# Two groups of stores in a one-layer encoder step: prepared w_out operands stored from ScalarE's queue one step behind, partial outputs stored right behind each pair's last sum

## The chip, the cores and the metric

The kernel runs on one core of a Trainium2 chip. The metric is the device time of one launch in microseconds. Each number on the profile is from one profiled execution of that launch.

The core has five engines that run their own instruction streams in order: TensorE (PE; its weight loads are listed apart as PEld), VectorE (DVE), ScalarE (ACT), GpSimd (POOL) and SyncE (SP). SP, ACT and POOL can start DMA transfers. An engine that issues a transfer waits in its own stream until the data to be moved is ready.

## The reference, cut to what matters

One layer of an encoder over 4096 prompt rows and 32 sample rows of width 1024, in float32:

```python
h = rmsnorm(x, norm_g)
u, v, z_a, xb, z_b = jnp.split(h @ w_in, 5, axis=-1)               # each 1024 wide
a = u * chunk_mlp(layernorm(v), w_spatial, b_spatial) * silu(z_a)  # 8 heads, 128 x 128 mixing
b = pool_mix(xb_with_past, ...) * silu(z_b)                        # trailing windows 2, 4, 8, 16
y = x + concat([a, b], -1) @ w_out                                 # w_out is 2048 x 1024
return rmsnorm(y, final_g), ...                                    # and three small states
```

## The kernel before, in words

All large products are Strassen-like: a product of two-by-two blocks is made of seven block products (q = 0 to 6) in place of eight. Each operand is split in a rounded upper half and the rest (hi and lo), and a block product is 12 matmuls: four blocks of the contraction, each hi x hi, hi x lo and lo x hi. One block product is called a step here.

The program has three stages.

1. Norms, the v columns, and the operands made of the normalised rows. The operands go to DRAM (`xops`), the v rows to `v_all`.
2. Four groups of 1024 tokens, each with 16 sets of 128 columns: 8 gate sets (z and u) and 8 pooling sets (x_B folded with the pooling weights, and z_B). The results, branch outputs transposed, go to DRAM (`abT`).
3. The product with w_out, in two halves of its rows: z = 0 for branch a, z = 1 for branch b. A pair is 256 token rows. The 16 pairs of z = 0 write partial sums to DRAM (`part`), the 16 pairs of z = 1 read them back, add, normalise and write the output. The last two pairs of z = 0 keep their sums on chip for the first two of z = 1.

In stages 2 and 3 the operands that the matmuls take as weights are made on the fly. `prepare` runs through the list of steps five ahead of the multiplication (`LEAD = 5`). For each step it issues due loads and then runs the step's preparation: ACT rounds the block to hi (line 120), DVE subtracts to get lo (line 82), and for some q DVE forms sums first (line 116). Each operand lies in a buffer `wop`, of which there are seven. ACT also copies block products out of PSUM (lines 168, 173 and 175), and DVE adds others (line 166).

w_out's own operands (class `OutWeights`, one for each half z and row block k, so eight of them with seven operands each, 56 in all) are prepared during stage 2, beside a step's own preparation, one every second or every third step. They too go through a `wop` buffer and are then stored to DRAM (`wops`), from which stage 3 loads them. The store is issued by SP right behind the preparation (line 631), in the same queue as the loads of raw weights (line 897) and v rows (line 890). The buffer is free when the store has landed.

In stage 3 a pair's sums lie in two tiles `y`. After the last step of a pair, DVE adds the last product (line 703). `finish` stores `y` to `part` from POOL (line 714); before the change it is called in the third step of the next pair, and for the first pair right behind its own last step.

The order in which the instructions of each engine stand is not the order of the code alone: a scheduler places them by its own estimate of when each is ready, engine by engine, and a few are held in the order of the code (`keep_in_program_order`).

Of the kernel before, what the change touches and what calls it, by code (L numbers as in the profile page):

```python
# [8 lines left out]
F32 = mybir.dt.float32  # L9
# [22 lines left out]
NQ = 7  # L32
# [4 lines left out]
def stream_step(ctx: ExitStack, tc, x_prompt, x_sample, state_pool, norm_g, w_in, ln_v_g, ln_v_b,  # L37
# [9 lines left out]
    nc = tc.nc  # L47
# [30 lines left out]
    def small(tag, n, rows=P):  # L78
        return smallp.tile([P, 8], F32, tag=tag, name=tag)[:rows, :n]
# [32 lines left out]
    def weight_ops(a1, a2, b1, b2, sums, dst, in_order=False):  # L112


        keep = {}
        less = lambda o, x, y: nc.vector.tensor_tensor(o, x, y, ALU.subtract)  # L116

        def split(q, src):
            hi, lo, *then = dst(q)
            pair = nc.scalar.copy(hi, src), lo_part(lo, src, hi)  # L120
            if q == 0 and in_order:
                for ins in pair:
                    tc.keep_in_program_order(ins)
            if behind:
                behind.pop()
                tc.keep_in_program_order(pair[0])
            for step in then:
                step()

        def third():  # L130
            keep[1], keep[2] = sums(), sums()
            less(keep[1], b1, a1)
            less(keep[2], b2, keep[1])
            split(2, keep[2])

        def fourth():
            less(b1, b2, b1)
            split(3, b1)

        def last():  # L140
            less(a2, a2, keep[2])
            split(6, a2)

        return [lambda: split(0, a1), lambda: split(1, a2), third, fourth, lambda: split(4, keep[1]),
                lambda: split(5, b2), last]
# [67 lines left out]
    def pool(name, bufs, stack=ctx, **kw):  # L213
        return stack.enter_context(tc.tile_pool(name=name, bufs=bufs, reuse_waits="tile", **kw))
# [4 lines left out]
    with ExitStack() as ph:  # L219
# [138 lines left out]
        class Past:  # L358


            def load(self):
                self.st = half(), half()
                for z in range(2):
                    nc.gpsimd.memset(self.st[z][:HALO], 0.0)
                    nc.sync.dma_start(self.st[z][1:HALO], state_pool[0, 0, :, z * 512:(z + 1) * 512])
# [234 lines left out]
    def raw_tile(dt=F32):  # L600
        return raw_p.tile([P, D], dt, tag="raw", name="raw")

    def weight_tile():
        return op_p.tile([P, 2, 4, P], F32R, tag="wop", name="wop")
# [6 lines left out]
    def load_out_weights(z, q):  # L611
        w_slots[z, q] = t = slot()[:, :4 * D].rearrange("p (k h n) -> p k h n", k=4, h=2)
        nc.sync.dma_start(t.bitcast(F32), wops[z, q].rearrange("p k (h n) -> p k h n", h=2))

    class OutWeights:


# [3 lines left out]
        def load(self):  # L621
            v = []
            for i in range(2):
                raw = raw_tile()
                nc.sync.dma_start(raw, w_out_v[8 * self.z + 4 * i + self.k])
                v.append(raw.rearrange("p (s c e) -> p s c e", s=2, e=P))

            def dst(q):
                t = weight_tile()
                out = wops[self.z, q, :, self.k, :]  # L630
                store = lambda: nc.sync.dma_start(out, t.rearrange("p h k t -> p (h k t)").bitcast(F32))
                return t[:, 0], t[:, 1], store

            self.prep = weight_ops(v[0][:, 0], v[1][:, 0], v[0][:, 1], v[1][:, 1], sum_tile, dst)

# [172 lines left out]
    with ExitStack() as ph:  # L808
# [225 lines left out]
        groups = []  # L1034
# [4 lines left out]
        n_sets = len(groups)  # L1039
# [23 lines left out]
        def prepare(upto):  # L1063

            nonlocal done
            while done < min(upto, len(steps)):
                while loads and loads[0][0] <= done + (AHEAD if done < first[id(groups[n_sets][0])] + 7 else 6):
                    loads.pop(0)[2].load()
                s, q = steps[done]
                s.prep[q]()  # L1070
                if done in beside:
                    w, q = beside[done]
                    w.prep[q]()
                done += 1
# [25 lines left out]
        for n in range(n_sets):  # L1100
            g, order = groups[n], orders[n]
# [48 lines left out]
    with ExitStack() as ph:  # L1150
        y_p = pool("y_p", 6, ph)
        ps_more = pool("ps_more", 2, ph, space=bass.MemoryType.PSUM)

        def y_tile():
            return y_p.tile([P, D], F32, tag="y", name="y")

        def more_tile():
            return ps_more.tile([P, 512], F32, tag="more", name="more")

        def spare_tile():  # L1160
            return spare_p.tile([P, D], F32, tag="spare", name="spare")


        def sum_words():
            return sum_p.tile([P, 512], F32, tag="sum", name="few")

        def few_columns():
            t = sum_words()
            return [t[:, i * DEC:(i + 1) * DEC] for i in range(2)]

        state = FewRows(lambda k: stk[:, k * m_edge + EXT:(k + 1) * m_edge],
                        lambda k: w_in[0, k * P:(k + 1) * P, 3 * D:4 * D], few_columns, KT // 2 - 1)
        outs = FewRows(lambda k: abT[k, :, SEQ:], lambda k: w_out_v[k], few_columns, KT - 1)

        def state_end():
            low = raw_tile()
            few_sums(low[:DEC], state.acc, sum_words)
            nc.sync.dma_start(st_prompt[0, 0], low[DEC - POOL_STATE:DEC])
            nc.sync.dma_start(st_sample[0, 0], low[EXT - POOL_STATE:EXT])

        def outs_end():
            y, low = raw_tile()[:DEC], raw_tile()[:DEC]
            nc.sync.dma_start(y, xs)
            few_sums(low, outs.acc, sum_words)
            nc.vector.tensor_tensor(y, low, y, ALU.add)
            ss, a = small("nb", 1, DEC), small("na", 1, DEC)
            junk = sum_p.tile([P, 2 * 512], BF16, tag="sum", name="junk")[:DEC]
            nc.scalar.activation(junk, y, AF.Square, accum_out=ss)
            nc.vector.tensor_scalar(a, ss, 1.0 / D, EPS, ALU.mult, ALU.add)
            r = rsqrt(a, 1, DEC)  # L1190
            nc.vector.scalar_tensor_tensor(y, y, r, f_bc[:DEC], ALU.mult, ALU.mult)
            nc.gpsimd.dma_start(ys, y)

        def sample_rows():

            vs, gb, bb = [raw_tile()[:DEC] for _ in range(3)]
            nc.sync.dma_start(vs, v_smp)
            nc.sync.dma_start(gb, ln_v_g[0].partition_broadcast(DEC))
            nc.sync.dma_start(bb, ln_v_b[0].partition_broadcast(DEC))
            nc.vector.tensor_tensor(gb, vs, gb, ALU.mult)  # L1200
            nc.vector.tensor_tensor(gb, gb, bb, ALU.add)
            nc.gpsimd.dma_start(v_sample[0, 0], gb)

        aside = {n_sets + 4 + 2 * j: (state, j, state_end) for j in range(4)}
        aside.update({n_sets + i: (outs, j, outs_end) for j, i in enumerate((5, 7, 9, 11, 17, 19, 21, 23))})
        kept, ended = [], None
        for n in range(n_sets, len(groups)):
            g, order = groups[n], orders[n]
            for s in g if n > n_sets else ():
                s.begin(kept.pop(0) if kept else None)  # L1210
            if g[0].z and ended is None:
                f_bc = spare_tile()
                nc.sync.dma_start(f_bc, final_g.partition_broadcast(P))
            for m, (s, q) in enumerate(order):
                at += 1
                prepare(at + LEAD)
                if m == 0 and n in aside:
                    aside[n][0].load(aside[n][1])
                if n == n_sets + 12 and m == 2:
                    sample_rows()  # L1220
                s.multiply(q)
                if n == n_sets and s is g[0] and q == NQ - 1:
                    s.finish()
                if m == 2 and ended:
                    for x in ended:
                        x.finish()
                if s is g[-1] and n + 1 < len(groups) and groups[n + 1][0].stage != s.stage:
                    load_out_weights(1, q)
                if m == 6 and n in aside:
                    few, j, end = aside[n]  # L1230
                    few.multiply(j, more_tile() if j == 0 else None)
                    if j == few.last:
                        end()
            ended = g[1:] if n == n_sets else g
            if g[0].z == 0 and groups[n + 1][0].z == 1:
                kept, ended = [x.y for x in g], None


# [27 lines left out]
```

## Time and profile before

| | |
|---|---|
| time, median of 3 runs | 2337.78 us (2337.70 to 2338.09) |
| profiled execution, its own time | 2337.89 us |
| its span, first to last instruction | 2336.0 us |
| PE busy | 2317.2 us (99%) |
| DVE busy | 1774.6 us (76%) |
| ACT busy | 889.3 us (38%) |
| POOL busy | 229.2 us (10%) |
| mean granted TensorE clock | 0.999 |
| stores of w_out's operands (line 631) | 56 of 512 KB, in SP's queue |
| stores of partial outputs (line 714) | 28 of 512 KB, in POOL's queue |

Busy shares are means over stages that have different limits. A group row gives busy time, the mean duration of one instruction, and the idle time of the engine ahead of it with what ended that. A wait is put down to what came last. A DMA row gives the time of its issue on the engine, and in the chain of waits the time until it landed. Idle time of an engine that nothing waits for costs nothing.

### The profile page before, as it was taken

To read this page: it belongs to the slowest core of one execution; us is meant where nothing else is said; L and a number is where in the kernel's file an instruction comes from. 1 tells how busy PE (TensorE), PEld (TensorE's weight loads), DVE (VectorE), ACT (ScalarE), POOL (GpSimd) and SP (SyncE) were. 2 spreads that over 40 slices of the span, in tenths; PEclk is the share of its full clock that TensorE was granted. 3 is DMA by queue.
4 is the path that set the end of the run, shared out by engine and by line. 5 is a ranking of instruction groups with operands and counts; after the bars stand their busy time and mean duration, and the time that the engine had idled before them with its cause. 6 is when DMAs were issued, how large, how long until landed. Compare 5 with 4: busy or idle time off the path is not lost.

```text
span 2336.0 us, 32648 instructions
## 1 busy us (share of the span) xinstructions
PE 2317.2 (99%) x11936; PEld 1964.7 (84%) x11936; DVE 1774.6 (76%) x3285; ACT 889.3 (38%) x1596; POOL 229.2 (10%) x412
## 2 busy tenths in 40 slices
PE   8999999999999999999999999999999999999998
PEld 7888888888888888888877899999988777887887
DVE  6888777867887777868668877768776666588887
ACT  7544444334433333433334333334322222233343
POOL 1010000100112000111001211102110000000000
PEclk9999999999999999999999999999999999999999
DMA  8879977335447433483454474435584656846552
GB/s 316 310 269 280 281 244 251 111 108 189 145 170 271 147 127 130 129 328 120 164 164 149 165 276 146 143 94 173 192 323 163 211 201 198 342 163 202 178 167 91
DMA packets 329544, 457.42 MB, mean 196 GB/s; under 512 B 21964, under 2 KB 249932, under 8 KB 326696
## 3 DMA queue, kind: packets, MB, share of 16 engines
q1 hardware_dynamic: 277832, 366.91, 46.9%
q0 software_dynamic: 22288, 73.48, 8.4%
q10 hardware_dynamic: 29264, 14.94, 2.3%
q8 instruction: 94, 1.54, 0.3%
q14 instruction: 66, 0.54, 0.1%
HBM read 286.07 MB, written 169.21 MB: 195 GB/s over the span
## 4 chain that ended last, share of the span: by engine, by line
PE 94%; DMA 3%; DVE 2%; issue 1%; ACT 0%; SPq 0%; DVEq 0%; ACTq 0%
PE acc L194 64%; PE acc L691 8%; PE acc L692 8%; PE acc L693 8%; PE sp L939 2%; PE tr L452 1%; DMA wops<-wop 1%; DMA vt<-in_w_in_dram 1%; DVE wop L82 1%; DMA raw<-abT 1%; PE more L202 1%; DMA op<-in_w_in_dram 0%; PE acc L269 0%; PE acc L202 0%; DMA raw<-in_w_in_dram 0%
## 5 line engine op out<-in xcount | busy, mean ns | idle before, releaser
L194 PE MATMUL acc<-slot,wop 128*128 128x512 f32 (+1 forms) x6720 | 1260.1, 348 | 2.9 <-ACT t L173 1.0
L194 PEld LDWEIGHTS acc<-slot,wop 128*128 128x128 f32 x6720 | 1080.3, 188 | 163.2 <-DVE t L166 6.2
L82 DVE TENSOR_TENSOR wop<-raw,wop 128x512 fp32r<-128x512 f32 x520 | 355.8, 686 | 99.0 <-ACT wop L120 96.3
L120 ACT CAST wop<-raw 128x512 fp32r<-128x512 f32 x360 | 222.8, 622 | 349.2 <-PE acc L194 259.7
L691 PE MATMUL acc<-slot,wop 128*128 128x512 f32 x892 | 348.7, 391 | 1.8 <-DVE y L703 1.8
L693 PE MATMUL acc<-slot,wop 128*128 128x512 f32 x892 | 347.1, 389 | 0.0
L692 PE MATMUL acc<-slot,wop 128*128 128x512 f32 x892 | 347.0, 389 | 0.0
L194 PE MATMUL acc<-slot,op 128*128 128x512 f32 x1344 | 323.5, 395 | 0.1
L194 PEld LDWEIGHTS acc<-slot,op 128*128 128x128 f32 x1344 | 247.6, 188 | 51.8 <-DVE op L82 0.5
L703 DVE TENSOR_TENSOR y<-acc,y 128x512 f32<-128x512 f32 x235 | 159.1, 687 | 128.0 <-PE acc L693 126.9
L166 DVE TENSOR_TENSOR t<-acc,t 128x512 f32<-128x512 f32 (+1 forms) x320 | 185.7, 582 | 85.8 <-ACT t L175 44.9
L691 PEld LDWEIGHTS acc<-slot,wop 128*128 128x128 f32 x892 | 167.4, 188 | 47.0 <-ACT wop L656 11.9
L656 ACT CAST wop<-raw 128x512 fp32r<-128x512 f32 x160 | 99.6, 622 | 259.7 <-PE acc L693 251.9
L693 PEld LDWEIGHTS acc<-slot,wop 128*128 128x128 f32 x892 | 167.4, 188 | 35.2
L692 PEld LDWEIGHTS acc<-slot,wop 128*128 128x128 f32 x892 | 167.5, 188 | 34.2
L82 DVE TENSOR_TENSOR wop<-sum,wop 128x512 fp32r<-128x512 f32 x208 | 142.5, 686 | 57.6 <-ACT wop L120 57.0
L952 POOL DMA_DIRECT2D abT<-t x128 | 69.2, 541 | 822.3 <-DVE t L964 607.9
L120 ACT CAST wop<-sum 128x512 fp32r<-128x512 f32 x144 | 89.4, 622 | 152.6 <-PE acc L194 98.4
L975 DVE TENSOR_TENSOR t<-t 128x527 f32<-128x527 f32 (+3 forms) x160 | 111.0, 697 | 0.5
L656 ACT CAST wop<-sum 128x512 fp32r<-128x512 f32 x64 | 39.9, 623 | 131.6 <-PE acc L693 102.4
L116 DVE TENSOR_TENSOR sum<-raw 128x512 f32<-128x512 f32 x72 | 49.5, 687 | 36.8 <-DMA raw<-in_w_in_dram 34.9
L175 ACT COPY t<-acc 128x512 f32<-128x512 f32 (+1 forms) x80 | 40.1, 503 | 91.0 <-PE acc L194 90.5
(199 smaller groups left out, 1866.1 us busy)
## 6 DMA issues: line engine op xcount, KB each, us to landing
raw<-in_w_in_dram SPq DMA_DIRECT2D x110, 512.0 KB, 4.3
xops<-op SPq DMA_DIRECT2D x72, 512.0 KB, 5.7
abT<-t POOLq DMA_DIRECT2D x128, 256.0 KB, 3.7
raw<-abT SPq DMA_DIRECT2D x64, 512.0 KB, 4.7
slot<-xops SPq DMA_DIRECT2D x30, 1024.0 KB, 9.6
wops<-wop SPq DMA_DIRECT2D x56, 512.0 KB, 3.3
slot<-wops SPq DMA_DIRECT2D x14, 2048.0 KB, 9.9
xt<-in_x_prompt_dram SPq DMA_DIRECT2D x32, 512.0 KB, 4.4
```

The costliest lines, as they stand in the source:

```text
L82: return nc.vector.tensor_tensor(out, src, hi.bitcast(F32), ALU.subtract)
L116: less = lambda o, x, y: nc.vector.tensor_tensor(o, x, y, ALU.subtract)
L120: pair = nc.scalar.copy(hi, src), lo_part(lo, src, hi)
L166: add = lambda o, x, y: nc.vector.tensor_tensor(o, x, y, ALU.add)
L194: mm(acc, stationary(s, k), moving(m, k), start=fresh and n == 0, stop=n == len(terms) - 1, skip_group_check=True)
L656: nc.scalar.copy(t[:, 0], src)
L691: mm(acc, x[:, 0, k, :], w[:, k, 0, c], start=fresh and k == 0, stop=False, skip_group_check=True)
L692: mm(acc, x[:, 0, k, :], w[:, k, 1, c], start=False, stop=False, skip_group_check=True)
L693: mm(acc, x[:, 1, k, :], w[:, k, 0, c], start=False, stop=k == 3, skip_group_check=True)
L703: nc.vector.tensor_tensor(y, self.acc[bank], y, ALU.add)
L952: nc.gpsimd.dma_start(abT[row, :, t0:t0 + HALF], t[:, :HALF])
L975: tt(nxt[:, lo:HALO + m], s[:, lo:HALO + m], s[:, lo - step:HALO + m - step], ALU.add)
```

## The change

Two edits. The store of a prepared w_out operand is put in a list instead of being issued, and `prepare` empties the list at the start of the next step, ahead of that step's preparation; it is issued from ACT's queue. And `finish` of every pair of z = 0, apart from the last two, is called right behind the pair's last step.

```diff
+    stores = []
+
     class OutWeights:
 ...
             def dst(q):
                 t = weight_tile()
                 out = wops[self.z, q, :, self.k, :]
-                store = lambda: nc.sync.dma_start(out, t.rearrange("p h k t -> p (h k t)").bitcast(F32))
-                return t[:, 0], t[:, 1], store
+                store = lambda: nc.scalar.dma_start(out, t.rearrange("p h k t -> p (h k t)").bitcast(F32))
+                return t[:, 0], t[:, 1], lambda: stores.append(store)
 ...
                     loads.pop(0)[2].load()
+                while stores:
+                    stores.pop(0)()
                 s, q = steps[done]
                 s.prep[q]()
 ...
                 s.multiply(q)
-                if n == n_sets and s is g[0] and q == NQ - 1:
+                if s.z == 0 and groups[n + 1][0].z == 0 and q == NQ - 1:
                     s.finish()
 ...
-            ended = g[1:] if n == n_sets else g
+            ended = g if g[0].z else None
             if g[0].z == 0 and groups[n + 1][0].z == 1:
-                kept, ended = [x.y for x in g], None
+                kept = [x.y for x in g]
```

Lines below the edits move by two, and by four at the end: the store is line 633 in the changed kernel, the raw loads are 899 and 892.

ACT where the first w_out operands are made, in gate sets of the first token group. `wop_4871` and `wop_4922` are w_out's operands; `wop_4919`, `wop_4940` and the others are the sets' own; `acc` is PSUM. Before:

```order
L173 COPY t_4859<-acc_4804 128x512
L120 CAST wop_4871<-raw_4710 128x512
L120 CAST wop_4892<-sum_4889 128x512
L120 CAST wop_4919<-raw_4683 128x512
L175 COPY t_4907<-acc_4804 128x512
L120 CAST wop_4922<-raw_4712 128x512
L120 CAST wop_4940<-sum_4888 128x512
L120 CAST wop_4963<-raw_4683 128x512
```

With the change:

```order
L173 COPY t_4859<-acc_4804 128x512
L120 CAST wop_4871<-raw_4710 128x512
L633 DMA wops_70<-wop_4871 128x1024
L120 CAST wop_4892<-sum_4889 128x512
L120 CAST wop_4919<-raw_4683 128x512
L175 COPY t_4907<-acc_4804 128x512
L120 CAST wop_4922<-raw_4712 128x512
L633 DMA wops_70<-wop_4922 128x1024
L120 CAST wop_4940<-sum_4888 128x512
L120 CAST wop_4963<-raw_4683 128x512
```

The stores stand in ACT's stream directly behind the copies of the same operands. `wop_4919` takes the buffer of `wop_4871` in both orders and waits for its store.

SP at the same place, before:

```order
L625 DMA raw_4712<-in_w_out_dram 128x1024
L631 DMA wops_70<-wop_4871 128x1024
L897 DMA raw_4839<-in_w_in_dram 128x8x128
L631 DMA wops_70<-wop_4922 128x1024
L897 DMA raw_4841<-in_w_in_dram 128x8x128
L631 DMA wops_70<-wop_4970 128x1024
L890 DMA raw_4838<-v_all_72 128x1024
```

With the change:

```order
L627 DMA raw_4712<-in_w_out_dram 128x1024
L899 DMA raw_4839<-in_w_in_dram 128x8x128
L899 DMA raw_4841<-in_w_in_dram 128x8x128
L892 DMA raw_4838<-v_all_72 128x1024
L899 DMA raw_5009<-in_w_in_dram 128x8x128
```

The loads keep their order and have no stores between them.

ACT in a gate set of the last token group, where a step's columns come in two parts (264 wide) and so has two PSUM copies. `wop_12946` is the last operand of one row block of w_out, and `wop_13023`, which takes its buffer, is a set's own. Before:

```order
L120 CAST wop_12946<-raw_12225 128x512
L923 ACTIVATE t_12925<-t_12925 128x264
L120 CAST wop_12986<-raw_12709 128x512
L923 ACTIVATE t_12925<-t_12925 128x264
L173 COPY t_13001<-acc_12912 128x264
L120 CAST wop_13023<-raw_12709 128x512
L173 COPY t_13001<-acc_12927 128x264
```

With the change:

```order
L120 CAST wop_12946<-raw_12225 128x512
L633 DMA wops_70<-wop_12946 128x1024
L925 ACTIVATE t_12925<-t_12925 128x264 x2
L120 CAST wop_12986<-raw_12709 128x512
L173 COPY t_13001<-acc_12912 128x264
L120 CAST wop_13023<-raw_12709 128x512
L173 COPY t_13001<-acc_12927 128x264
```

The copy to `wop_13023` still stands ahead of the second copy out of PSUM. TensorE's instructions stand in the same order in both kernels, and so do POOL's, ACT's, DVE's and SP's in stage 3, the stores of partial outputs among them; DVE's and ACT's order shifts in places of stage 2.

## The prediction

> **What bounds the kernel now.** I read the page's busy times first, then TensorE's busy time stretch by stretch, then the waits, then the chain of waits around the two places that came out of that.
>
> ```profile
> span 2336.0 us, 32648 instructions
> PE 2317.2 (99%) x11936; PEld 1964.7 (84%) x11936; DVE 1774.6 (76%) x3285; ACT 889.3 (38%) x1596; POOL 229.2 (10%) x412
> ```
>
> TensorE (PE) is busy in all but 18.8 us of the span, so the only time that a change of queues can win is inside those 18.8 us. The stretches say where they are (columns: stretch, its length, PE busy and matmuls in it, granted clock, DMA share, GB/s):
>
> ```profile
> 0.00:60.00 60.00, 53.29 (x285) 0.97 0.88 319
> 380.00:400.00 20.00, 19.05 (x85) 1.00 0.87 305
> 1260.00:1280.00 20.00, 19.10 (x85) 1.00 0.65 218
> 1480.00:1500.00 20.00, 18.98 (x158) 1.00 0.39 122
> 1740.00:1760.00 20.00, 18.52 (x82) 1.00 0.57 188
> 1960.00:1980.00 20.00, 19.66 (x90) 1.00 0.58 178
> 2320.00:2336.00 16.00, 8.58 (x50) 0.90 0.17 67
> ```
>
> The losses are 6.71 us at the start, 0.95 at 380, 0.90 at 1260, 1.02 at 1480, 1.48 at 1740, 0.34 at 1960 and 7.42 us at the end; together 18.82, which is all of it. The stores that the change moves run only from 524.9 to 1624.0 us (their row is below), so the start and the loss at 380 are out of reach, and the tail is the last pair's own arithmetic. The waits tell what ends the two losses in between:
>
> ```profile
> ACT wop L120 <- PE acc L194: 358.0, 204, 3.8
> ACT wop L120 <- DMA wops<-wop: 74.2, 45, 5.8
> PE acc L194 <- ACT t L173: 1.0, 1, 1.0
> PE acc L194 <- DVE t L166: 0.9, 1, 0.9
> SPq L631 <- DVE wop L82: 168.6, 41, 8.7
> ```
>
> ScalarE (ACT) waited 45 times, 74.2 us in all, for a store of prepared w_out operands to land, because its next rounding copy (line 120) reuses the buffer that the store reads. PE has one wait of 0.9 us and one of 1.0 us in this part. The chain of waits ties the two together:
>
> ```profile
> 1267.89 6.30 DMA wops<-wop
> ...
> 1274.29 0.63 ACT wop L120
> ...
> 1278.08 0.70 DVE t L166
> ...
> 1473.88 7.58 DMA wops<-wop
> ...
> 1482.06 0.38 ACT t L173
> ...
> 1482.49 1.73 PE acc L194 x12
> ```
>
> Both PE losses begin with a store that needed 6.30 and 7.58 us to land. ACT stood still until then, and the copies and sums out of PSUM behind it were late. Of 74.2 us of ACT waiting, 0.90 + 1.02 = 1.92 us reached PE, that is 2.6%.
>
> **Why those two were late.** This is the timeline ahead of the first:
>
> ```profile
> 1264.85 0.36 SPq L897 DMA_DIRECT2D raw<-comb  x1
> 1265.32 0.52 SPq L897 DMA_DIRECT2D raw<-in_w_in_dram  x1
> 1266.67 0.52 SPq L897 DMA_DIRECT2D raw<-comb  x1
> 1267.18 0.68 DVE L82 TENSOR_TENSOR wop<-sum,wop 128x512 fp32r<-128x512 f32 x1
> 1274.29 0.62 ACT L120 CAST wop<-sum 128x512 fp32r<-128x512 f32 x1 [3.15 <-DMA wops<-wop]
> ```
>
> The lower half of the operand (line 82) ended at 1267.86 and SyncE (SP) issued the store at 1267.89. The issue was not late: three loads of 512 KB stood ahead of the store in the same queue. The wait of 168.6 us in 41 of 56 stores says the same from SP's side: mostly SP is there first and stands, with the raw loads behind the store standing too.
>
> **The change, part by part.** First, the 56 stores move to ACT's queue. The rows that price it:
>
> ```profile
> L631 SPq DMA_DIRECT2D wops<-wop x56: 319/327/929, 524.9 to 1624.0; - x56
> DMA to landing us min/median/max: 2.6/3.3/7.6
> ...
> L517 ACTq DMA_DIRECT2D v_all<-vt x28: 366/366/403, 88.3 to 356.7; - x28
> DMA to landing us min/median/max: 3.3/5.6/7.3
> ```
>
> Issue: 56 x 0.366 = 20.5 us of ACT's time. Although the code says one step behind, the rows of the change put each store one or two ACT instructions behind its own rounding copy, so ACT also stands until line 82 has run: 56 x 0.69 us (the 0.68 us row above) = 38.6 us if VectorE (DVE) is free. Together 59 us. The work that hides them is ACT's own waiting, 358.0 us in 204 waits for PE at line 120, and ACT's load of 38%. I cost them at 0; if the cover is gone they cost PE what ACT's waits have cost it so far, 2.6% of 59 = 1.5 us. Nothing else queues behind the store on ACT than rounding copies (five steps ahead of their use) and PSUM copies; those are the second rival.
>
> Landing: the store now stands in a queue of its own, not behind the loads. The trace does not show these stores there. The ends are its own median, 3.3 us, and the slowest store that ACT's queue landed in the first stage, 7.3 us. The loss at 1480 goes when the landing is under 7.58 - 1.02 = 6.56 us, the one at 1260 when it is under 6.30 - 0.90 = 5.40 us. I take 3.3 us, the row of the same transfer; the 5.6 us median of ACT's queue belongs to a stage with a DMA share near that of the 0.87 row, against 0.65 and 0.39 at the two places. At 3.3 us both losses go: -1.92 us. At 7.3 us neither does: 0. A step earlier or later in the store's issue matters little, since the issue was immediate.
>
> The Trainium skill, "DMA: Bandwidth & Descriptors", section "Issuing engines are not separate DMA queues", speaks against this: whichever engine starts a DMA, it runs on the same 16 DMA engines and interleaves, and a second issuing engine saves only issue time. By that sentence the landings stay and the sum is 0 instead of -1.92. The same page, section "Queues, rings and completion order", says that each DMA engine takes turns between queue rows packet by packet, by which a store in its own row passes loads that are ahead of it in SP's. No run here shows which of the two carries.
>
> SP loses 56 issues and the waits of 168.6 us ahead of them. The raw loads behind them start earlier; no PE wait names a raw load in this part, so 0. What can come late next is the buffer of the rounding copy, still freed by the store's landing.
>
> Second, the partial sums. The rows of one pair:
>
> ```profile
> 1758.25 0.69 DVE L703 TENSOR_TENSOR y<-acc,y 128x512 f32<-128x512 f32 x1
> 1759.24 0.53 POOL L714 DMA_DIRECT2D part<-y  x1 [17.55 <-DVE y L703]
> ```
>
> GpSimd (POOL) had stood 17.55 us for this sum and issued the store 0.30 us behind its end. POOL has nothing else to run there, so the store already goes out behind the last sum; writing it earlier in the program moves it in no queue. Cost and gain 0, also for PE, whose instructions stand in the same order in both kernels.
>
> **Sum.** The profiled execution took 2337.89 us, 1.9 us around its span and 0.1 us above the median of the runs, 2337.78. 2337.89 - 1.92 + 0 = 2335.97: I say 2336.0 us, 0.08% less. A measurement of this kernel can tell about 0.2%, 4.7 us, from no change, so the forecast is no change that counts.
>
> **The rivals.** (1) The landings stay long, because the same bytes share the same DMA engines, and ACT's new standing is added: 2337.9 + 0 to 1.5, so 2337.9 to 2339.4 us. For it: a store frees the buffer only a few ACT instructions later, and this stays so in the changed order; 45 waits averaged 1.65 us even where SP was early. Against it: only 2 of 45 reached PE, and both stood behind a burst of loads.
>
> (2) Slower: the store in ACT's in-order stream holds back a copy out of PSUM. The rows:
>
> ```profile
> 1228.32 5.46 PE acc L194 x24
> 1270.03 0.59 ACT L173 COPY t<-acc 128x512 f32<-128x512 f32 x1 [2.32 <-PE acc L194]
> 1246.86 1.14 ACT L120 CAST wop<-raw 128x512 fp32r<-128x512 f32 x2
> 1249.51 0.67 DVE L82 TENSOR_TENSOR wop<-raw,wop 128x512 fp32r<-128x512 f32 x1
> 605.00:660.00 55.00, 55.00 (x245) 45.53 (x244) 48.56 (x84) 23.39 (x40) 10.39 (x13) 1.00 0.44 137
> ```
>
> A step of 12 matmuls is 5.46 / 2 = 2.73 us. The bank that is copied after one step is written again in the step after next, so a copy of 0.59 us may start 2.14 us late. A store that waits for DVE takes the lag plus 0.37, so it decides from a lag of 1.77 us. Such a lag occurs: the copies that ended at 1248.00 had their second lower half at 1250.18, 2.18 us. Then PE loses 2.18 + 0.37 - 2.14 = 0.41 us. In the changed order 20 of the 56 stores stand directly ahead of a copy out of PSUM; if all 20 lag so, 20 x 0.41 = 8.2 us: 2346.1 us. For it: beside the pooling sets (the 605 to 660 row) DVE is busy 48.56 of 55 us, so lags are likely there. Against it: waits of up to 5.8 us at line 120 have mostly cost PE nothing, and the lag of 2.18 us is from a place where DVE also had the sample rows' sums to do.
>
> (3) Faster by more than 0.2%: after the first store PE loses only 0.90 + 1.02 + 1.48 + 0.34 = 3.74 us ahead of the tail, so even all of it gives 2334.2 us.
>
> That one half does nothing, the partial stores, is already in the sum.
>
> **How the numbers follow.** Forecast 0.58; rival 1 0.30; rival 2 0.07; rival 3, or a gain in a place that I count as out of reach, 0.02; small shifts elsewhere 0.03. The range goes from 2335.2, which is the forecast with twice the scatter of the three runs (0.4 us) below it, to 2339.4, where rival 1 ends; it leaves out rival 2 and 3 and a part of the small shifts, under 2 in 10. Faster by over 0.2%: 0.02. Slower by over 0.2%: 0.07, rival 2. The same: 0.91.
>
> **What would show it.** Right: the wait of ACT's line 120 for the stores falls well under 74.2 us, the slowest landing of the 56 stores is under 6 us, and the stretches 1260 to 1280 and 1480 to 1500 are busy throughout. SP's waits at the store are gone, and POOL's 24 partial stores start as far behind the sums as before. Wrong by rival 1: landings of 6 us and more remain, and PE still loses some 2 us there. Wrong by rival 2: new PE waits at line 194 that ACT's PSUM copies or DVE's sums end, most of them where DVE is fullest, with ACT waiting at the store for line 82. PE losses in other places, from the order in which the scheduler now puts DVE's work, would make the sum wrong in a way that I have not priced.

## The result: 0.6% slower, and the profile after

The changed kernel takes 2350.9 us (median; 2349.35 to 2353.8), the kernel before 2337.78 us beside it. The ratio is 1.0060, with a 95% interval of 1.0049 to 1.0071. The forecast was 2336.0 us, its range ended at 2339.4. So the change costs 13 us, and the forecast had the sign and the size wrong.

The page of the changed kernel (lines have moved by two: the store is line 633, the load of raw weights 899, of v rows 892, the partial store 716):

```profile
span 2347.6 us, 32592 instructions
PE 2318.6 (99%) x11936; PEld 1963.6 (84%) x11936; DVE 1774.3 (76%) x3285; ACT 887.8 (38%) x1596; POOL 226.9 (10%) x412
```

No engine has more to do. PE's busy time is 1.4 us above that of before, its idle time 29.0 us where it was 18.8. TensorE's stretches of the changed kernel say where the idle time is (columns as in the prediction; the first row is the whole stretch in which the moved stores run):

```profile
525.00:1640.00 1115.00, 1103.03 (x6052) 957.58 (x6052) 834.88 (x1402) 415.06 (x750) 143.02 (x240) 1.00 0.49 168
560.00:580.00 20.00, 16.87 (x81) 13.60 (x80) 13.67 (x23) 6.93 (x13) 1.08 (x2) 1.00 0.49 158
820.00:840.00 20.00, 17.54 (x84) 14.12 (x83) 14.38 (x25) 7.18 (x14) 1.08 (x2) 1.00 0.51 169
940.00:960.00 20.00, 18.88 (x84) 15.35 (x83) 16.14 (x27) 7.38 (x14) 4.16 (x5) 1.00 0.56 183
1140.00:1160.00 20.00, 18.13 (x87) 14.66 (x85) 13.57 (x23) 7.78 (x14) 1.08 (x2) 1.00 0.55 185
1160.00:1180.00 20.00, 18.65 (x92) 15.54 (x96) 12.78 (x21) 6.40 (x11) 1.08 (x2) 1.00 0.24 79
1260.00:1280.00 20.00, 20.00 (x90) 16.39 (x89) 19.93 (x46) 9.50 (x16) 7.38 (x5) 1.00 0.45 147
1280.00:1300.00 20.00, 19.02 (x84) 15.34 (x84) 18.27 (x31) 7.91 (x14) 3.24 (x5) 1.00 0.56 189
1480.00:1500.00 20.00, 19.02 (x158) 18.80 (x157) 13.57 (x25) 7.57 (x18) 2.77 (x6) 1.00 0.57 185
```

From 525 to 1640 us TensorE idles 1115.00 - 1103.03 = 11.97 us. Before it was 1115.00 - 1113.09 = 1.91 us, by the same view:

```profile
525.00:1640.00 1115.00, 1113.09 (x6153) 970.24 (x6152) 846.96 (x1424) 421.76 (x761) 148.99 (x243) 1.00 0.50 169
```

So 10.06 of the 11.6 us by which the span grew (2347.6 - 2336.0) are new idle time of TensorE in this stretch, in places where it lost nothing before (PE is busy for 20.00 of 20.00 us in these stretches of the kernel before): 3.13 us at 560, 2.46 at 820, 1.12 at 940, 3.22 at 1140 to 1180. The loss at 1260 is gone and one of 0.98 us stands at 1280; the loss at 1480 stayed.

The row of the moved stores, then the waits that changed most:

```profile
L633 ACTq DMA_DIRECT2D wops<-wop x56: 326/327/400, 524.4 to 1636.4; - x56
...
DMA to landing us min/median/max: 2.6/4.3/7.4
```

```profile
ACT wop L120 <- DMA wops<-wop: 92.2, 48, 5.3
DVE sum L116 <- DMA raw<-in_w_in_dram: 58.0, 26, 5.3
ACT t L175 <- DVE wop L82: 12.2, 7, 2.6
ACT wop L120 <- DVE wop L82: 10.5, 4, 3.0
PE acc L194 <- DVE t L166: 8.7, 6, 2.6
SPq L899 <- DVE wop L82: 391.4, 79, 21.8
```

The median landing of a store went from 3.3 to 4.3 us. ACT's waits for stores went from 74.2 to 92.2 us, DVE's waits for raw weights from 34.9 to 58.0 us. The waits of 168.6 us of SP at the store are gone, and its waits for line 82 at the raw loads have grown from 311.2 to 391.4 us: line 82 is the last reader of a raw buffer, so it frees it for the next load.

The chain of waits ahead of the loss at 560 shows the loop (start, duration, what):

```profile
536.71 5.13 DMA wops<-wop
...
541.86 0.63 ACT wop L120
...
543.84 4.47 DMA wops<-wop
...
548.39 0.63 ACT wop L120
...
549.04 1.30 DVE wop L82 x2
...
550.37 4.39 DMA wops<-wop
...
563.34 0.61 DVE wop L82
563.97 7.51 DMA raw<-in_w_in_dram
...
576.54 0.61 DVE t L166
...
577.19 3.02 PE acc L194 x12
```

Rounding copy, lower half, store, landing, and the next rounding copy into the same buffer: one round takes 543.84 to 550.37, 6.5 us, and two steps of TensorE 5.46 us by a row of the prediction (in gate sets two of seven steps also have the eight matmuls of line 941, 1.05 us). The loop was there before too, and tight: the seven stores of this row block were issued from 524.85 to 562.67, 37.8 us, and now from 524.36 to 563.98, 39.6 us. The operands are prepared five steps ahead; each slow round uses up some of that lead, until TensorE stands ahead of 577.19 us. The last link there is a raw load of 7.51 us, not a store. Whether late loads or late stores make the loss is taken up at the end of experiment 7.

### The profile page after: what moved, and what is told of

Its sections match the earlier page's. It is cut to its first block, busy times and chain, and to the rows that moved or that the text cites. A ratio compares the mean times of both kernels' runs of the same rounds, so it can differ in the third digit from the quotient of the medians.

```text
span 2347.6 us, 32592 instructions
## 1 busy us (share of the span) xinstructions
PE 2318.6 (99%) x11936; PEld 1963.6 (84%) x11936; DVE 1774.3 (76%) x3285; ACT 887.8 (38%) x1596; POOL 226.9 (10%) x412
## 4 chain that ended last, share of the span: by engine, by line
PE 87%; DMA 6%; DVE 4%; ACT 1%; issue 1%; SPq 0%; ACTq 0%; DVEq 0%
PE acc L194 58%; PE acc L693 8%; PE acc L695 8%; PE acc L694 8%; DMA wops<-wop 4%; PE sp L941 2%; DVE wop L82 2%; PE tr L452 1%; DMA raw<-in_w_in_dram 1%; DMA op<-in_w_in_dram 1%; ACT wop L120 1%; DMA raw<-abT 1%; PE more L202 1%; DVE t L166 0%; DVE sum L116 0%
## 5 line engine op out<-in xcount | busy, mean ns | idle before, releaser
L693 PEld LDWEIGHTS acc<-slot,wop 128*128 128x128 f32 x892 | 167.4, 188 | 46.5 <-ACT wop L658 11.6
L175 ACT COPY t<-acc 128x512 f32<-128x512 f32 (+1 forms) x80 | 40.1, 503 | 98.9 <-PE acc L194 83.5
```

The costliest lines, as they stand in the source:

```text
L693: mm(acc, x[:, 0, k, :], w[:, k, 0, c], start=fresh and k == 0, stop=False, skip_group_check=True)
```

## What sets the landing: a load that starts with the store

The timelines of the two kernels at the same store, the fifth of the first row block. Before:

```profile
550.98 0.32 SPq L631 DMA_DIRECT2D wops<-wop  x1
551.39 0.39 SPq L897 DMA_DIRECT2D raw<-in_w_in_dram  x1
554.08 0.62 ACT L120 CAST wop<-sum 128x512 fp32r<-128x512 f32 x1 [2.84 <-DMA wops<-wop]
```

And with the change:

```profile
550.17 0.37 SPq L899 DMA_DIRECT2D raw<-in_w_in_dram  x1
550.37 0.33 ACTq L633 DMA_DIRECT2D wops<-wop  x1
554.78 0.62 ACT L120 CAST wop<-sum 128x512 fp32r<-128x512 f32 x1 [2.88 <-DMA wops<-wop]
```

Before, the load of 512 KB stood behind the store in SP's queue and was issued 0.41 us after it; ACT went on 3.10 us after the store's issue. With the change SP no longer stands at the store, the load goes 0.20 us ahead of it, and ACT goes on after 4.41 us. At the last store of the block the lower half that ends at 563.95 us releases both: the load is issued at 563.97 and the store at 563.98, and the store needs 7.37 us where it had needed 5.60 (a second load had gone 1.2 us ahead in both kernels).

I read this off the timelines for all 56 stores, by the load nearest in time:

| | before | changed |
|---|---|---|
| stores with no load within 2.5 us | 22, landing 2.67 us | 22, landing 2.62 us |
| a load 0.15 to 2.5 us behind, none ahead | 8, landing 3.15 us | 0 |
| a load behind and another ahead | 7, landing 5.6 us | 0 |
| a load ahead, or within 0.15 us | 19, landing 5.04 us | 34, landing 4.59 us |

(Landing here is the median of the time from the store's issue to the copy that waited for it, where one waited.) The 15 stores that had a load behind them all have it at the same moment now, within 0.2 us. For 13 of these ACT waited in both kernels; their landings grew by 1.19 us in the median, the six with no other load beside them from 3.07 to 3.19 us to 4.38 to 4.57. The five with a load 0.42 to 0.44 us ahead became 0.3 to 0.8 us faster, since the load no longer gets that start. So what the store won by leaving SP's queue is smaller than what it lost.

That is the theory to be tested (**B**, the loads). Its rivals: **A**, ScalarE's standing at the store for line 82 and the issue itself hold back its copies; **C**, either cost reaches the sets' own operands only because all share seven buffers; **D**, the scheduler's other order of VectorE (153 of 3287 instructions stand elsewhere) costs by itself.

## The experiments

### 1. ScalarE stands, the store stays in SyncE's queue

```diff
# kernel before, OutWeights.load
-                return t[:, 0], t[:, 1], store
+                touch = lambda: nc.scalar.copy(small("touch", 1, 1), t[:1, 1, 0, :1].bitcast(F32))
+                return t[:, 0], t[:, 1], store, touch
```

> The kernel before, its stores in SyncE's queue as they were, and one tiny ScalarE copy of one element of the lower half behind each store's place, so that ScalarE stands in its in-order stream until VectorE's line 82 has run, as it does at the store in the changed kernel (the store's own issue of 0.33 us is left out, a copy of one element stands for it). Theory A, the standing costs: ScalarE's PSUM copies and next rounding copies come late, the time goes up by most of the 13 us, to 2346 to 2352 us, with new TensorE losses at about 560 and 820. Theory B, the landing costs: the loads, which SyncE no longer holds behind a store, run beside the store and it lands 1 us later; here SyncE still holds them, so the time stays at 2336 to 2340 us and the store's median landing at 3.3 us.

Measured: 2339.83 us, ratio to before 1.0007 (0.9998 to 1.0017).

```profile
ACT touch L632 <- DVE wop L82: 62.8, 51, 3.4
525.00:1640.00 1115.00, 1113.13 (x6148) 969.88 (x6147) 847.04 (x1422) 428.07 (x818) 149.55 (x243) 1.00 0.51 169
```

ScalarE stood 62.8 us in 51 waits for the lower half, as long as in the changed kernel, where its idle time straight ahead of the 56 store issues adds up to 62.6 us in the trace. TensorE's busy time in the stretch is that of before. Apart from the 56 tiny copies every engine's order is that of before. So the standing is not the main cause: by the interval it is worth at most 0.17%. The stores' own issue on ScalarE is left out here; experiments 2 and 5 cover it.

### 2. The changed kernel, with SyncE held behind the lower half

```diff
# changed kernel, OutWeights.load; mark is a scratch tensor in DRAM
-                return t[:, 0], t[:, 1], lambda: stores.append(store)
+                note = lambda: nc.sync.dma_start(mark[self.z, self.k, q:q + 1, :], t[:1, 1, 0, :16].bitcast(F32))
+                return t[:, 0], t[:, 1], lambda: stores.append(store), note
```

> The changed kernel, and behind each store's place a small DMA of SyncE's (64 bytes of the lower half into a scratch tensor), so that SyncE and the loads behind it stand until line 82 has run, as they did in the kernel before. ScalarE's stream is that of the changed kernel. Theory A, ScalarE's standing costs: nothing is given back, 2349 to 2353 us. Theory B, the loads run beside the store: they are held as before, the store's median landing falls from 4.3 to about 3.3 us, and the time to 2337 to 2341 us. In between: the small DMA's own 56 issues stand in SyncE's queue, and a landing between 3.3 and 4.3 us goes with a time between.

Measured: 2340.13 us, ratio 1.0011 (1.0001 to 1.0021).

```profile
525.00:1640.00 1115.00, 1113.22 (x6141) 968.02 (x6140) 846.30 (x1423) 420.41 (x761) 157.71 (x243) 1.00 0.50 169
```

```profile
550.04 0.33 ACTq L634 DMA_DIRECT2D wops<-wop  x1
550.36 0.40 SPq L901 DMA_DIRECT2D raw<-in_w_in_dram  x1
553.36 0.62 ACT L121 CAST wop<-sum 128x512 fp32r<-128x512 f32 x1 [1.80 <-DMA wops<-wop]
```

```profile
ACT wop L121 <- DMA wops<-wop: 55.3, 34, 4.6
ACT wop L121 <- DMA mark<-wop: 17.6, 6, 3.7
```

A DMA of 64 bytes in SyncE's queue gives back 10.8 of 13.1 us, with the store still in ScalarE's queue and ScalarE's order untouched (VectorE's shifts in a few places). The load is again 0.32 us behind the store, and ScalarE goes on after 3.32 us; in all, 9 stores have a load behind them alone and 6 a load on both sides (8 and 7 in the kernel before). ScalarE's waits for these buffers, those put down to the small DMA included, are 72.9 us, as before. This is what theory B expects and theory A excludes.

### 3. Half the bytes

```diff
# changed kernel; stage 3 loads the upper half into both halves of its tile
-                store = lambda: nc.scalar.dma_start(out, t.rearrange("p h k t -> p (h k t)").bitcast(F32))
+                store = lambda: nc.scalar.dma_start(out[:, :512], t[:, 0].rearrange("p k t -> p (k t)").bitcast(F32))
```

> The changed kernel with half the store: only the upper half of each operand is stored (256 KB in place of 512), and stage 3 loads the upper half into both halves of its tile, so the lower halves are left out of the last stage's products. The order, ScalarE's standing for line 82 and the queues stay. Theory A, the standing costs: 2348 to 2352 us, since ScalarE still stands and issues. Theory B, the landing costs: it falls by 1 us or more, the loop from one rounding copy to the next in the same buffer falls under TensorE's pace of some 6 us, and the time falls to 2335 to 2340 us.

Measured: 2337.25 us, ratio 0.9997 (0.9988 to 1.0006).

```profile
ACT wop L120 <- DMA wops<-wop: 40.3, 22, 4.0
525.00:1640.00 1115.00, 1113.49 (x6155) 970.32 (x6153) 847.08 (x1425) 422.99 (x761) 156.71 (x243) 1.00 0.47 156
```

This kernel leaves the lower halves out of the last products, so it is a measurement only. The whole loss goes with the shorter stores. A reservation: the order of the engines shifted too here (239 of ScalarE's and 333 of VectorE's instructions), and 9 stores again have their load behind, so this run alone would not tell size from order. It does show that halving the store gains nothing over the kernel before.

### 4. A buffer of their own for w_out's operands, in the changed kernel and in the one before

```diff
-    op_p = pool("wop_p", 7)
+    op_p = pool("wop_p", 6)
+    own_p = pool("own_p", 1)
...
-                t = weight_tile()
+                t = own_p.tile([P, 2, 4, P], F32R, tag="own", name="own")
```

> The changed kernel with one buffer kept for w_out's operands alone, and six in place of seven for the sets' own operands, the same SBUF in all. A rounding copy of w_out then waits for the store of w_out's operand before it, issued a step earlier or more; no copy of a set's own operand waits for a store. Theory C, that the shared buffer, taken again by the next rounding copy, passes the store's landing on to the sets' own operands: ScalarE's waits at line 120 for stores fall from 92 us by more than half and the time to 2335 to 2341 us. If the losses come from ScalarE's standing alone (theory A), the time stays at 2348 to 2352 us. If six buffers for the sets' own operands are too few, it goes above the changed kernel.

> The kernel before with one buffer kept for w_out's operands and six in place of seven for the sets' own, as in the split of the changed kernel, which took 2344.5 us. Theory C, that a landing reaches TensorE only through the shared buffer: without it the two queues cost the same, so 2342 to 2347 us here too, the price of the split itself. If the queue still tells with split buffers, because loads that land late reach the sums directly, this one is 3 us or more faster, 2336 to 2341 us.

Measured: 2344.53 us, ratio 1.0030 (1.0019 to 1.0041), for the changed kernel; 2339.64 us, ratio 1.0012 (1.0003 to 1.0022), for the kernel before. The stretch for the one and for the other:

```profile
525.00:1640.00 1115.00, 1110.45 (x6111) 964.59 (x6110) 846.22 (x1414) 417.93 (x754) 139.08 (x243) 1.00 0.50 169
```

```profile
525.00:1640.00 1115.00, 1112.81 (x6153) 969.69 (x6152) 849.97 (x1423) 420.90 (x760) 135.62 (x243) 1.00 0.50 169
```

With split buffers ScalarE's queue costs 0.30 - 0.12 = 0.18% instead of 0.60%; the two intervals just overlap. So the shared buffer seems to carry much of the damage, as theory C says, but probably not all, and my expectation for the changed kernel (2335 to 2341) was missed. The split itself costs 0.12%, and it reorders ScalarE and VectorE widely. What carries the rest is open. The split does not take the landings out of ScalarE's stream: the copies of w_out's own operands still wait there for stores, 61.0 us in the changed kernel and 58.3 in the one before. Nor is it shown that late loads carry it: VectorE's waits for raw weights are 51.6 and 47.6 us.

### 5. GpSimd's queue in place of ScalarE's

```diff
# changed kernel
-                store = lambda: nc.scalar.dma_start(out, t.rearrange("p h k t -> p (h k t)").bitcast(F32))
+                store = lambda: nc.gpsimd.dma_start(out, t.rearrange("p h k t -> p (h k t)").bitcast(F32))
```

> The changed kernel with the 56 stores in GpSimd's queue in place of ScalarE's: ScalarE's order is that of the kernel before, instruction for instruction, and ScalarE stands at no store, while SyncE and its loads are as free as in the changed kernel. Theory A, ScalarE's standing and issuing costs: the time goes back to 2336 to 2340 us. Theory B, the loads released by the same lower half (line 82) run beside the store and make it land late: it stays at 2346 to 2352 us, with a median landing of some 4.3 us and ScalarE's waits for stores near 90 us. Theory D, that the scheduler's other order of VectorE costs (153 of 3287 instructions stand elsewhere in the changed kernel, 35 here): back to 2336 to 2340 us too. Stores that GpSimd issues later than ScalarE did (it stands for other things in between) would come on top.

Measured: 2356.12 us, ratio 1.0086 (1.0069 to 1.0102).

```profile
ACT wop L120 <- DMA wops<-wop: 116.7, 51, 5.4
525.00:1640.00 1115.00, 1103.24 (x6044) 956.69 (x6043) 832.66 (x1397) 413.85 (x749) 170.12 (x293) 1.00 0.49 168
```

ScalarE stands at no store, its order is that of before, VectorE's differs from before in 35 instructions, and TensorE loses as much in the stretch as with the change, 11.76 us (the profiled execution is the fastest of the four, 2351.14 us). This is the run that theories A and D can't live with: the loss comes with SyncE's freedom, not with what ScalarE carries. Here 27 stores have a load only ahead or together, 6 one on both sides, and none one behind alone.

The loss is larger than theory B's 2346 to 2352 us, and ScalarE's waits for stores are 116.7 us instead of near 90, so the expectation was missed on that side. GpSimd issues a store 0.30 us behind the end of its lower half in the median, ScalarE 0.03, so the load that the same lower half releases has that much more start; the 27 stores land in 5.37 us in the median, 34 in 4.59 in the changed kernel. GpSimd's issue is also slower, 0.537 us against 0.327. How much each adds is not shown.

### 6. Both edits with the stores left in SyncE's queue, and the second edit alone

```diff
# changed kernel, the first edit without its queue
-                store = lambda: nc.scalar.dma_start(out, t.rearrange("p h k t -> p (h k t)").bitcast(F32))
+                store = lambda: nc.sync.dma_start(out, t.rearrange("p h k t -> p (h k t)").bitcast(F32))
```

> Both edits as in the changed kernel, one step behind and the partial stores early, but the 56 stores stay in SyncE's queue. VectorE's order then differs from the kernel before in 20 of 3287 instructions. Theories A and B both say the kernel before's time, 2336 to 2340 us, since ScalarE has no store and SyncE holds the loads. If the deferral or the partial stores cost anything by themselves, it shows here: 2342 us and more.

> The second edit alone: partial sums written in the program right behind each pair's last sum, all else as before. Every engine's instructions stand in the order of the kernel before. Every theory says no change: 2336.5 to 2339 us, GpSimd's 24 partial stores at the same distance from their sums. A difference over 0.1% would mean that the same order can come out at different times from something that the order does not show.

Measured: 2337.61 us, ratio 1.0004 (0.9994 to 1.0013), and 2337.01 us, ratio 1.0001 (0.9991 to 1.0010). Neither "one step behind" nor the early partial stores cost or gain anything that these runs can tell. The loss belongs to the one word that names the queue.

### 7. Two other times for SyncE's hold

Experiment 2 holds SyncE until the lower half. These hold it until the upper half, 0.7 us earlier, and until the store has landed.

```diff
# on the kernel of experiment 2: until the upper half
-                note = lambda: nc.sync.dma_start(mark[self.z, self.k, q:q + 1, :], t[:1, 1, 0, :16].bitcast(F32))
+                note = lambda: nc.sync.dma_start(mark[self.z, self.k, q:q + 1, :], t[:1, 0, 0, :16].bitcast(F32))
# until the landing
-                return t[:, 0], t[:, 1], lambda: stores.append(store), note
+                note = lambda: nc.sync.dma_start(mark[self.z, self.k, q:q + 1, :], out[:1, :16])
+                return t[:, 0], t[:, 1], lambda: stores.extend((store, note))
```

> The changed kernel with the small DMA of SyncE's on the upper half in place of the lower: SyncE and the loads stand until ScalarE's rounding copy (line 120) has run, some 0.7 us before the store can go, and not until the lower half (line 82), as where the hold took 2340.1 us. If what counts is that the store goes first and a load that the same lower half releases goes 0.3 to 0.4 us behind it, this hold comes too early to set that order, and most of the loss stays: 2345 to 2352 us. If any standing of SyncE's at every operand is enough to space the loads: 2338 to 2341 us.

> The changed kernel, and behind each store a small DMA of SyncE's that reads 64 bytes of what the store wrote, so that SyncE and the loads behind it stand until the store has landed. ScalarE's order is that of the changed kernel, instruction for instruction, and VectorE's but for 3 of 3287. If the losses come from loads that run beside the store: fewer stores share the DMA engines with a load than in any kernel so far, ScalarE's waits at line 120 for stores fall below the 74.2 us of the kernel before and the time to 2336 to 2340 us, unless the loads, some 3 us later each, are now late themselves, which would show as VectorE's waits at line 116 for raw loads above the 58.0 us of the changed kernel and a time of 2342 us or more. If they come from ScalarE's standing: 2348 to 2353 us.

Measured, upper half: 2349.20 us, ratio 1.0049 (1.0034 to 1.0064). The same 64-byte DMA, 0.7 us earlier, and most of the loss is back, 11.5 of 13.1 us. Its timeline at the store compared above:

```profile
552.66 0.38 SPq L901 DMA_DIRECT2D raw<-in_w_in_dram  x1
553.03 0.33 ACTq L634 DMA_DIRECT2D wops<-wop  x1
558.20 0.62 ACT L121 CAST wop<-sum 128x512 fp32r<-128x512 f32 x1 [3.63 <-DMA wops<-wop]
```

Measured, landing: 2381.73 us, ratio 1.0186 (1.0169 to 1.0203).

```profile
553.62 0.53 SPq L901 DMA_DIRECT2D raw<-in_w_in_dram  x1
555.10 0.33 ACTq L634 DMA_DIRECT2D wops<-wop  x1
561.74 0.62 ACT L121 CAST wop<-sum 128x512 fp32r<-128x512 f32 x1 [5.12 <-DMA wops<-wop]
```

```profile
ACT wop L121 <- DMA wops<-wop: 126.8, 48, 6.5
DVE sum L117 <- DMA raw<-in_w_in_dram: 60.6, 26, 6.1
```

This expectation failed. I thought that such a hold would keep the loads off the stores. It keeps them off the store just issued, and sends them out into the next one: no store has its load behind it, and those with a load ahead or together land in 5.87 us in the median, against 4.59 in the changed kernel. VectorE's waits for raw weights are barely above those of the changed kernel (60.6 and 58.0 us), so later loads are not the main reason. But this kernel differs in more than when the load goes. Three stores with a load 0.60 us ahead land in 5.1, 4.9 and 4.9 us in the changed kernel, and in 6.0, 6.3 and 5.9 us here at the same distance. And of the 47.0 us by which its span exceeds that of before (2383.0 and 2336.0), 17.2 are not idle time but TensorE's busy time (2334.4 us instead of 2317.2), with a mean granted clock of 0.993 in place of 0.999. The record shows neither why the clock was lower nor what the 56 small reads themselves cost.

Put side by side, the one store gives a series from five kernels, of which the first four differ mainly in when the load goes:

| kernel | load's issue against the store's | ScalarE goes on after |
|---|---|---|
| before | 0.41 us behind | 3.10 us |
| hold until the lower half | 0.32 us behind | 3.32 us |
| changed | 0.20 us ahead | 4.41 us |
| hold until the upper half | 0.37 us ahead | 5.17 us |
| hold until the landing | 1.48 us ahead | 6.64 us |

The last row is not the load's start alone, by what was said above. Nor does a longer start always hurt more: in the kernel before, three stores with a load 1.71 us ahead let ScalarE go on after 3.3 to 3.4 us.

And over whole kernels, the number of stores with a load behind them and none ahead parts the runs. So do ScalarE's waits for stores, and VectorE's waits for raw weights do not:

| kernel | ratio to before | stores with a load behind only | ACT's waits for stores | DVE's waits for raw weights | TensorE idle, 525 to 1640 us |
|---|---|---|---|---|---|
| before | 1 | 8 | 74.2 us | 34.9 us | 1.91 us |
| 1, ScalarE stands | 1.0007 | 8 | 76.4 us | 43.2 us | 1.87 us |
| 2, hold until the lower half | 1.0011 | 9 | 72.9 us (with the small DMA's) | 40.1 us | 1.78 us |
| 6, both edits, SyncE's queue | 1.0004 | 8 | 75.6 us | 55.7 us | 3.01 us |
| 6, second edit alone | 1.0001 | 8 | 78.0 us | 36.7 us | 1.70 us |
| changed | 1.0060 | 0 | 92.2 us | 58.0 us | 11.97 us |
| 5, GpSimd's queue | 1.0086 | 0 | 116.7 us | 51.5 us | 11.76 us |
| 7, hold until the upper half | 1.0049 | 0 | 91.3 us | 38.1 us | 9.42 us |
| 7, hold until the landing | 1.0186 | 0 | 126.8 us | 60.6 us | 31.20 us |

So late loads alone do not make the loss, though the chain at 560 ended in one. With both edits in SyncE's queue VectorE waits for raw weights nearly as long as in the changed kernel, 55.7 us, and no loss is seen; with the hold until the upper half it waits 38.1 us, about as in experiment 2, and most of the loss is there. The split kernels of experiment 4 stand in between, with 11 such stores at a ratio of 1.0012 and 3 at 1.0030. In the kernel of experiment 3, with 9, the stores are half as long.

A kernel that beats both did not come out of this. TensorE idles 1.91 us in this stretch in the kernel before, 0.08% of the time, so there is nothing that a better place for these stores could win and a measurement could show.

## Why the prediction was wrong

**What bounds the kernel** was read rightly: TensorE at 99%, little to win. That made the question "what can be lost", and the forecast spent its working on what could be won.

**The landing term** failed: "I take 3.3 us, the row of the same transfer ... At 3.3 us both losses go: -1.92 us." It measured 4.3 us, and 4.4 to 4.6 where it counts. The row of 3.3 us was a mixture: 2.67 us alone, 3.15 with a load behind, 5.04 with one ahead. The forecast noted that loads ahead of the store in SP's queue made it late. It did not ask which stores had a load *behind* them, and by the timeline of before 15 of the 56 have. Leaving the queue takes a store past the loads ahead, and takes the loads behind past the store.

**The step that hid it** is the one on SyncE: "The raw loads behind them start earlier; no PE wait names a raw load in this part, so 0." The 168.6 us for which SP stood at the stores were costed as a wait that goes away. They were an order: a load behind a store could not go until the store had gone. The cost of losing that order is what the hold until the lower half gives back, 10.8 us.

The rule that I weighed, of the Trainium skill's "DMA: Bandwidth & Descriptors", section "Queues, rings and completion order" (DMA engines take turns between queue rows packet by packet), agrees with these landings: stores with a load some 0.43 us ahead became 0.3 to 0.8 us faster in a queue of their own, stores with a load 0.4 us behind became 1.2 us slower in the median. I applied it only to the loads ahead. It does not tell the whole: in experiment 2 store and load stand in two queues as well, and with the load again 0.3 us behind the landing is back at 3.3 us, so what the store loses it loses with its start. By the same page of the Trainium skill, section "Issuing engines are not separate DMA queues", only issue time is saved; as a bound on the gain that was right, and 0 as the loss was my reading, not the page's.

**The conversion of 2.6%** was an average used as a price. ACT's waits for stores grew by 92.2 - 74.2 = 18.0 us and TensorE's idle time in the stretch by 10.06 us: 56% of the added wait, not 2.6%. (Other waits grew too, so 56% is a comparison of two sums and not a price.) My reading, which no run tests by itself, is that up to the kernel before the five steps of lead absorbed most waits, and that little of it was left: the two losses that the prediction quoted are places where it had run out.

**ScalarE's standing**, costed at 0 with a bound of 1.5 us, was about right: 0.07%, 1.6 us, by experiment 1, whose interval includes none. It was right with wrong terms: ScalarE stood 62.6 us where 38.6 were taken, and the issue took 0.327 us, not 0.366. Nor do only rounding copies and PSUM copies queue behind the store: directly behind 4 of the 56 stands an activation of line 925.

**The partial stores**, costed at 0, were right: the second edit alone is 1.0001, and POOL's 24 waits for their sums are 213.6 us, 213.7 before.

**Rival 1** looked at the right thing, the landings, and had the wrong price: it let them stay, where they grew. **Rival 2** had the right side and the wrong mechanism. Its price of 8.2 us came from ScalarE's stream; with ScalarE's stream as before and the store on GpSimd the loss is no smaller. Its sign came half true, which misleads: the new waits of TensorE are ended by ScalarE's copies (line 168) and VectorE's sums (line 166), as named, but not where VectorE is fullest. From 560 to 580 VectorE is busy 13.67 of 20 us, in the pooling row of the prediction 48.56 of 55.

Of the signs named in advance, ACT's wait rose instead of falling, the slowest landing was 7.4 us instead of under 6, and 1480 was not busy throughout; SP's waits at the store went and the partial stores kept their distance, as said. These signs tell that the landing term had failed, not why.

## What to carry to other kernels

An engine that stands at a transfer in its queue is also what keeps the transfers behind it back. Before moving a transfer out of an in-order queue, list what stands behind it, when that will now start, and whether one event (here the lower half, line 82) releases both. If the moved transfer frees a buffer that the next step needs, its landing beside the transfers that will now start with it is the price to use, and a median over all its instances, most of them in other company, is not. And where the bound engine is busy 99%, do not price the next microsecond of delay by the share of earlier delays that reached it: here that share was 2.6%, and over half of what was added.

## What I had not expected of the hardware

A head start of a few tenths of a microsecond between two transfers of 512 KB changes the landing by more than a microsecond: at the store compared above, 3.1 to 3.3 us with the load 0.3 to 0.4 us behind the store, 4.4 us with it 0.2 us ahead, 5.2 us with it 0.4 us ahead. Others agree: in the kernel before, four stores with a load 0.41 us behind landed in 3.0 us, and five with one 0.42 to 0.44 us ahead in 4.8 to 5.2 us. It holds across queues (experiment 2 has store and load in different ones), so the time of issue decides there, not only the place in one queue. And a DMA of 64 bytes, in the right place of a queue, was worth 10.8 us of 13.1.
